# Pads between value-block tiles: moving twelve SBUF tiles under the 512-column products of an encoder block

## The chip, the core and the metric

The kernel runs on one core of one Trainium2 chip. The metric is the device time of one execution in microseconds (us). TensorE is PE in the profile (its loads of stationary operands are listed apart as PEld), VectorE is DVE, ScalarE is ACT, GpSimd is POOL, SyncE is SP.

## The reference, cut to what matters

One encoder block over 1024 tokens of width 1024. A normalised input `h` is multiplied by one wide matrix `w_in`; its columns feed three mixers (dilated windows, grouped-query attention, attention into a memory) and three gates each; the results are merged and projected once more.

```python
h = rms_norm(x, g_pre[layer])
a_qkv, bq, bk, bv, mq, ga, gb, gm, mg = jnp.split(h @ w_in[layer], split_at, axis=-1)
...
merged = gates[:, :, 0] * ya + gates[:, :, 1] * yb + gates[:, :, 2] * ym
out = merged @ w_out[layer]
x = x + rms_norm(out, g_post[layer])
```

Everything below is about `h @ w_in`: how the operands of a part of that product lie in SBUF.

## The kernel before, in words

Each factor of a float32 product is split into a high and a low part, and a product is three matmuls: high by high, high by low, low by high. A large product is cut once more, into 2 by 2 blocks that are combined by a Strassen-like scheme: seven products (A11, A12, S2, S3, S4, S1, A22 by B11, B21, T2, T3, B22, T1, T4), where S1 to S4 are sums of weight blocks and T1 to T4 differences of token blocks. One matmul takes 128 rows by 128 columns of a stationary operand, which a load (LDWEIGHTS) puts into the array beforehand, and streams 512 columns of a moving operand past it ("a product of 512 columns"), or 256 columns in some stages.

The "mega stage" runs from about 450 to 1050 us and has three loops. The first (line 1225) makes two thirds of the value projection: token blocks are stationary, weight blocks of 512 columns move. The second (line 1276) makes the last third in the same way with 256 columns. The third (`pair_product`, matmuls on line 1315) makes 25 pairs of units: weight blocks are stationary, token blocks of 512 columns move. A pair has seven block products of 12 matmuls (four k times three passes), so the third loop has 25 x 7 x 12 = 2100 matmuls. In this whole stage the order on every engine is written out by hand (`tc.manual_schedule`), and PE has the matmuls of one block product after the other in its queue. While one matmul streams, the load of the next matmul's stationary operand runs.

The pool `vb` lies at the right end of SBUF and holds, in order of declaration, the twelve tiles of `Rows` (4096 bytes per partition each: A21, A22, A11, A12, S1, S2, two each, named vA210 to vS21), then `vv`, `vy`, `vot`, `vgt`, `vrt`, `kT3x`. In the first loop the twelve tiles hold raw weight blocks, which are split into other tiles before a matmul reads them. Later their places are used again:

- `KT_PLACE` (line 1020) puts the split token blocks T3 (k = 0, 1) into vA220 and vA221 and T1 into vA110, vA111, vA210, vA211; they are stationary in the second loop and moving in the third.
- `k_block` (line 1073) puts the split weight blocks S2, S1, S3, A22, S4 of the third loop into vS10, vS11, vS20, vS21 in turn; they are stationary there.
- `k_own` (line 1063) splits A11 and A12 of the third loop into `wh` and `wl`, which lie elsewhere.
- `k_load` (line 1044) lands every second pair's raw weights in vA120 and vA121, which VectorE, ScalarE and GpSimd read.

The built program gives each tile its byte address within a partition. What matters here is the remainder of that address by 512 bytes, the size of one loaded operand's row (128 columns of 4 bytes). Before the change the tiles of all operands of the stage's matmuls, moving and stationary, have the remainder 480. "Distance" is, below, the start of the operand being loaded for the next matmul minus the start of the operand streaming in this one, modulo 512; all 2099 steps from one matmul to the next in the third loop, 335 in the second and 335 in the first have the distance 0. Elsewhere the kernel has pads already: one of 448 bytes ahead of the tiles xk (line 236; the memory operands mh and ml of line 526 take their places, remainder 416) and one of 64 bytes ahead of the tiles of the memory attention (line 557; mqh and mql, remainder 32). There, products of 256 columns have distances of 64.

Of the kernel before, what the change touches and what calls it, by code (L numbers as in the profile page):

```python
# [8 lines left out]
F32 = mybir.dt.float32  # L9
# [8 lines left out]
P = 128  # L18
# [15 lines left out]
def block(ctx: ExitStack, tc: tile.TileContext, x, xT, memT, cst, msk, bcst, tabA, gpost,  # L34
# [183 lines left out]
    def pool(name, side="left"):  # L218
        p = tc.tile_pool(name=name, bufs=1, side=side, reuse_waits="tile")
        return p, p.__enter__()  # L220
# [681 lines left out]
    vbp, vb = pool("vb", "right")  # L902
# [7 lines left out]
    class Rows:  # L910

        def __init__(self, nm):
            self.t = [vb.tile([P, 2, 512], F32, name=f"v{nm}{z}") for z in range(2)]

        def __getitem__(self, at):
            return self.t[at[1] // 2][:, at[1] % 2]
# [1446 lines left out]
```

## Time and profile before

| what | value |
|---|---|
| median of the runs of the kernel before | 1369.76 us (1369.28 to 1370.23, 2 runs) |
| the profiled execution's own time | 1369.01 us |
| its span, first to last instruction | 1367.2 us |
| granted TensorE clock | 0.998 |
| PE busy / DVE / ACT / POOL | 98% / 74% / 48% / 42% of the span |
| line 1315 on PE, share of the chain that ended last | 35% |

PE's busy time counts overlapping matmuls once. A matmul's record lasts longer than the distance from its start to the next one's start, since matmuls are pipelined; the rate of a stretch is therefore read from starts, or from the count of matmuls in a window: a window of length W that touches n records of length L holds (W + L)/n per matmul.

### The profile page before, as it was taken

What the parts mean: (1) busy time and instruction counts of PE and PEld (TensorE: products, weight loads), DVE (VectorE), ACT (ScalarE), POOL (GpSimd) and SP (SyncE); (2) the same over time, 40 slices, a digit from 0 to 9 for tenths busy, and PEclk for the clock granted to TensorE, in tenths of its full rate; (3) what the DMA queues carried; (4) which work ended last, traced back from release to release, by engine and by line L of the source; (5) the groups of instructions that cost most, each with busy time, mean ns of one, the idle gap of its engine ahead of it and who ended that gap; (6) DMA issues with size and microseconds to landing.
All of it is one profiled execution on the core that took longest, in us unless ns stands there. A gap on an engine that the chain in (4) does not pass through costs nothing.

```text
span 1367.2 us, 22887 instructions
## 1 busy us (share of the span) xinstructions
PE 1346.3 (98%) x8303; PEld 1087.8 (80%) x8303; DVE 1016.8 (74%) x1836; ACT 655.3 (48%) x1388; POOL 579.4 (42%) x443
## 2 busy tenths in 40 slices
PE   8999999999999999999999999999999999999997
PEld 7899986666666788988888888888888778768886
DVE  7868677777777498767777776687787666768977
ACT  7544465656655445333333343333335676763332
POOL 0516702676676200244465554565553134662003
PEclk9999999999999999999999999999999999999999
DMA  7356532322244579514333333322337778986455
GB/s 253 109 170 231 179 110 92 103 79 93 74 132 141 210 226 285 158 61 139 101 115 117 108 123 123 116 96 92 106 123 262 229 216 236 273 228 228 149 186 185
DMA packets 125490, 213.81 MB, mean 156 GB/s; under 512 B 32481, under 2 KB 64577, under 8 KB 125377
## 3 DMA queue, kind: packets, MB, share of 16 engines
q1 hardware_dynamic: 116064, 198.42, 45.6%
q10 hardware_dynamic: 9312, 13.93, 2.8%
q8 instruction: 65, 1.06, 0.3%
q14 instruction: 49, 0.39, 0.1%
HBM read 145.92 MB, written 66.38 MB: 155 GB/s over the span
## 4 chain that ended last, share of the span: by engine, by line
PE 81%; DVE 6%; DMA 5%; ACT 3%; issue 2%; POOL 2%; SPq 1%; DVEq 0%; ACTq 0%; POOLq 0%
PE s L1315 35%; PE d L1904 6%; PE s L2128 4%; PE ov L810 3%; PE sc L2046 3%; PE s L1276 3%; PE d L132 3%; PE d L130 3%; PE d L128 3%; PE s L1588 2%; PE tr L776 2%; PE s L794 2%; PE s L795 2%; DMA vrt<-rld 2%; PE d L2128 2%
## 5 line engine op out<-in xcount | busy, mean ns | idle before, releaser
L801 POOL TENSOR_TENSOR bl<-bl,bp 128x512 f32<-128x512 f32 x96 | 133.2, 1388 | 54.1 <-ACT bp L797 48.6
L1315 PE MATMUL s<-hh,vS 128*128 128x512 f32 x400 | 131.3, 390 | 0.0
L1315 PE MATMUL s<-vA,vS 128*128 128x512 f32 x450 | 106.1, 390 | 0.0
L91 DVE TENSOR_TENSOR vS<-vot,vS 128x512 fp32r<-128x512 f32 x75 | 89.4, 1193 | 19.9 <-ACT vS L90 19.9
L1315 PEld LDWEIGHTS s<-vA,vS 128*128 128x128 f32 x450 | 84.5, 188 | 17.5
L797 ACT ACTIVATE bp<-s 128x512 f32<-128x512 f32 x128 | 75.6, 596 | 43.8 <-PE s L795 42.7
L777 DVE TENSOR_REDUCE bn<-tr 128x1 f32<-128x512 f32 x128 | 84.9, 683 | 13.3 <-PE tr L776 11.9
L132 PE MATMUL d<-hh,wl 128*128 128x512 f32 x224 | 89.8, 401 | 0.4 <-DVE wl L91 0.4
L128 PE MATMUL d<-hh,wh 128*128 128x512 f32 x224 | 89.2, 398 | 0.0
L130 PE MATMUL d<-hl,wh 128*128 128x512 f32 x224 | 89.1, 398 | 0.0
L1315 PEld LDWEIGHTS s<-hh,vS 128*128 128x128 f32 x400 | 75.2, 188 | 15.5
L1600 ACT ACTIVATE pra<-pra,sts 128x192 f32<-128x192 f32 (+1 forms) x176 | 72.4, 414 | 13.2 <-DVE sts L1599 12.9
L1315 PE MATMUL s<-hh,wl 128*128 128x512 f32 x200 | 78.2, 391 | 0.0
L1315 PE MATMUL s<-hl,wh 128*128 128x512 f32 x200 | 78.0, 390 | 0.0
L1315 PE MATMUL s<-hh,wh 128*128 128x512 f32 x200 | 78.0, 390 | 0.0
L1315 PE MATMUL s<-hl,vS 128*128 128x512 f32 x200 | 77.9, 390 | 0.0
L1599 DVE CUSTOM_DVE_ANT_0 pra<-s,mask 128x192 f32<-128x192 f32 (+1 forms) x192 | 48.9, 309 | 34.1 <-PE s L1588 20.1
L1059 POOL TENSOR_TENSOR vot<-wr 128x512 f32<-128x512 f32 x13 | 22.2, 1707 | 112.3 <-DMA wr<-in_wu 112.3
L1319 ACT ACTIVATE vv<-s 128x512 f32<-128x512 f32 x50 | 29.9, 598 | 82.0 <-PE s L1315 48.1
L810 PE MATMUL ov<-bp,VS 128*64 128x512 f32 x256 | 58.5, 599 | 0.0
L1059 POOL TENSOR_TENSOR vot<-vot,vA 128x512 f32<-128x512 f32 x12 | 19.3, 1606 | 89.3 <-DVE vS L91 89.3
L128 PEld LDWEIGHTS d<-hh,wh 128*128 128x128 f32 x224 | 42.3, 189 | 13.2 <-issue 5.5
(626 smaller groups left out, 4007.0 us busy)
## 6 DMA issues: line engine op xcount, KB each, us to landing
wr<-in_wu SPq DMA_DIRECT2D x40, 512.0 KB
vA<-in_wu SPq DMA_DIRECT2D x24, 512.0 KB
qkd<-ko SPq DMA_DIRECT2D x96, 128.0 KB
wl<-thd SPq DMA_DIRECT2D x24, 512.0 KB
wos<-os SPq DMA_DIRECT2D x12, 512.0 KB
wr<-in_wbr SPq DMA_DIRECT2D x24, 256.0 KB
aq<-qkd SPq DMA_DIRECT2D x12, 512.0 KB
ak<-qkd SPq DMA_DIRECT2D x12, 512.0 KB
```

The costliest lines, as they stand in the source:

```text
L91: V.tensor_tensor(dst_l, src, dst_h.bitcast(F32), op=OP.subtract)
L128: PE.matmul(dst, wh[:, k, :], hh[k][:, t], start=k == 0, stop=False)
L130: PE.matmul(dst, wh[:, k, :], hl[k][:, t], start=False, stop=False)
L132: PE.matmul(dst, wl[:, k, :], hh[k][:, t], start=False, stop=k == 7)
L777: fp["last"] = V.tensor_reduce(st[i]["n"][:, j, c:c + 1], s, axis=AX.X, op=OP.min)
L797: A.activation(pp, s, AF.Exp, scale=-1.0)
L801: G.tensor_tensor(lsum[i % 2], lsum[i % 2], pp, op=OP.add)
L810: PE.matmul(o[e * 64:e * 64 + 64], VS[:, kt, kv], d.pop(kt), start=kt < 2, stop=kt >= NT - 2)
L1315: PE.matmul(BANK[n, c], a, b, start=k == 0 and q == 0 and not more, stop=k == 3 and q == 2, skip_group_check=c in "XW")
L1600: A.activation(src, src, AF.Exp, scale=-1.0, bias=bias, accum_out=sts[:, 1, h, T:T + 1])
L1904: PE.matmul(ps_, a, b, start=k == 0 and q == 0, stop=k == 3 and q == 2)
L2128: PE.matmul(dst[:, e[0]:e[1]], a, b, start=k == 0 and q == 0, stop=k == 3 and q == 2)
```

## The change

After each of the twelve tiles a small tile is allocated that nothing writes or reads: 32 bytes per partition after eleven of them, 384 bytes after vS11. Since the pool ends at a fixed place, the tiles declared later keep their addresses and the twelve move down: vS21 by 32 bytes, vS20 by 64, vS11 by 448, vS10 by 480, vA121 by 512, vA120 by 544, vA111 by 576, vA110 by 608, vA221 by 640, vA220 by 672, vA211 by 704, vA210 by 736.

```diff
     class Rows:
 
         def __init__(self, nm):
-            self.t = [vb.tile([P, 2, 512], F32, name=f"v{nm}{z}") for z in range(2)]
+            self.t = []
+            for z in range(2):
+                self.t.append(vb.tile([P, 2, 512], F32, name=f"v{nm}{z}"))
+                vb.tile([P, 96 if (nm, z) == ("S1", 1) else 8], F32, name=f"pad{nm}{z}")
```

No instruction is added, taken out or moved on any engine or queue, and no wait differs; the two programs differ in addresses alone. Distances of the built program after the change, counted over steps from one matmul to the next:

| loop (columns) | 0 | 32 | 64 | 96 to 288 | 288 to 448 | 448 (64 below) | 480 (32 below) |
|---|---|---|---|---|---|---|---|
| third, line 1315 (512) | 617 | 312 | 292 | 357 | - | 257 | 264 |
| second, line 1276 (256) | 263 | 0 | 0 | - | 72 | - | 0 |
| first, line 1225 (512) | 287 | 0 | 0 | - | 48 | - | 0 |

Within one block product of the third loop the distance stays the same or nearly so; it changes between block products.

## The prediction

> **What bounds the kernel now.** I read the chain that ended last, limited to the third loop of the mega stage, then the windows by stage, then who waited for whom there, and last single starts of matmuls.
>
> The chain from 572 to 1000 us:
>
> ```profile
> 2 pieces in order of time: start us, us, what
> 571.93 0.36 PE s L1276 x3
> 572.29 427.87 PE s L1315 x1886
> ```
>
> It is one unbroken piece of PE: 1886 matmuls in 427.87 us, 226.9 ns each, with no other engine in it. The windows of the same stretch, and two inside it (busy us and count per engine, in the order PE, PEld, DVE, ACT, POOL):
>
> ```profile
> 572.00:1000.00 428.00, 428.00 (x1890) 354.18 (x1889) 322.33 (x342) 157.36 (x248) 225.22 (x135) 1.00 0.35 111
> ...
> 580.00:780.00 200.00, 200.00 (x884) 165.46 (x883) 148.44 (x158) 73.55 (x115) 101.68 (x61) 1.00 0.35 111
> 780.00:980.00 200.00, 200.00 (x883) 165.51 (x882) 149.43 (x158) 73.51 (x114) 104.86 (x64) 1.00 0.34 108
> ```
>
> PE is busy throughout at the full granted clock (1.00); DVE works 322 of 428 us, ACT 157, POOL 225. (200 us + 0.39)/884 is 226.7 ns per matmul, in both halves alike. The other engines wait for PE or for one another; the longest waits there of ACT and POOL, each from its own list:
>
> ```profile
> ACT vS L90 <- PE s L1315: 85.0, 32, 4.8
> ```
>
> ```profile
> POOL vot L1059 <- DVE vS L91: 209.2, 54, 8.4
> ```
>
> So a nanosecond more or less per matmul of line 1315 goes into the time in full, up to the slack of DVE (106 us of 428), and nothing that the other engines do is late for PE. The question is only what the address of an operand does to the distance from one matmul's start to the next.
>
> **The change part by part.** Nothing is issued more or less, so there are only prices per product, and the trace of before has no steady run of 512-column products at a distance other than 0. I bound them by the 256-column products, where it has both.
>
> Durations by line, first of the second value loop (256 columns, distance 0), then of the memory keys (256 columns, distance mostly 64), then of the third loop (512 columns, distance 0); min/median/max in ns:
>
> ```profile
> L1276 PEld LDWEIGHTS s<-wh,hl x64: 187/193/193, 531.8 to 571.8; 128*128 128x128 f32 x64
> L1276 PE MATMUL s<-wh,hl x64: 282/284/284, 531.9 to 571.9; 128*128 128x256 f32 x64
> ```
>
> ```profile
> L526 PEld LDWEIGHTS d<-ml,wh x64: 187/188/193, 56.0 to 79.6; 128*128 128x128 f32 x64
> L526 PE MATMUL d<-ml,wh x64: 276/277/283, 56.1 to 79.7; 128*128 128x256 f32 x64
> ```
>
> ```profile
> L1315 PEld LDWEIGHTS s<-vA,vS x450: 187/188/188, 580.1 to 1041.2; 128*128 128x128 f32 x150
> L1315 PE MATMUL s<-vA,vS x450: 388/390/390, 580.3 to 1041.5; 128*128 128x512 f32 x150
> ```
>
> And the starts: a window that holds line 1276 alone, and eleven consecutive matmuls of line 526:
>
> ```profile
> 535.00:555.00 20.00, 20.00 (x169) 20.00 (x168) 13.88 (x19) 10.61 (x17) 0.00 (x0) 1.00 0.79 240
> ```
>
> ```profile
> 59.33 0.28 PE L526 MATMUL d<-mh,wh 128*128 128x256 f32 x1
> ...
> 60.46 0.28 PE L526 MATMUL d<-ml,wh 128*128 128x256 f32 x1
> ```
>
> At distance 0 a 256-column product takes (20 us + 0.284)/169 = 120.0 ns, at 64 it takes 1.13 us/10 = 113 ns; the loads at distance 0 are 4 to 5 ns longer (193 against 188). So addresses do seem to matter, by 7 ns, where the load of 128 columns and the stream of 256 both fill the whole step (PEld is busy 20.00 of 20.00 us in that window). Two things speak against carrying this over to 512 columns. There, the load has slack: PEld is busy 165.46 of 200 us, and its record is 188 ns, the short value, at distance 0. And 226.7 ns for 512 columns is twice 113 ns for 256 to within the rounding: 0.443 ns per column in both. I read that as a floor per column on which the 512-column products already stand at distance 0.
>
> One rule of the Trainium skill bears on this: "TensorE: Matmul & The Clock Gate", section "Part 2: What happens when you issue a matmul", says that TensorE has two independent SBUF read ports, so that loading the next weights takes no read bandwidth from the running matmul. By that rule the sum is zero for every distance. The 512-column rows agree, as far as they go; the 120 against 113 ns at 256 columns do not, unless something other than the distance separates those lines.
>
> The terms, each against the profiled execution's 1369.01 us (span 1367.2 us; the median of the runs, 1369.76, is 0.75 us above it):
>
> 1. Line 1315, 617 of 2099 steps keep the distance 0: nothing. 1482 steps change. Lower end: each gains what the 256-column products show, 7 ns, 1482 x 0.0067 = 9.9 us (with 120.0 - 113.3). Upper end: each is as slow as 512-column products are after a disturbance (next rows), 5.8 ns, 8.6 us lost. I take 0: the floor per column is the nearest row, being the same products on the same line.
>
> 2. Changes of distance between block products, new in this stage. The nearest rows are after a break of another kind, two transposes at 86.10 us between products of 512 columns, all at distance 0:
>
> ```profile
> 86.10 0.38 PE L514 MATMUL tr<-cs,kvt 128*128 128x128 f32 x2
> 86.24 0.48 PE L128 MATMUL d<-hh,wh 128*128 128x512 f32 x1
> 86.55 0.40 PE L130 MATMUL d<-hl,wh 128*128 128x512 f32 x1
> ...
> 88.41 0.39 PE L128 MATMUL d<-hh,wh 128*128 128x512 f32 x1
> ```
>
> The eight steps from 86.55 to 88.41 us take 232.5 ns each: 46 ns in all above 226.7 before the products settle. The other row is a change of distance itself, from 0 to 64 and to the memory scores:
>
> ```profile
> 173.57 0.39 PE L132 MATMUL d<-hh,wl 128*128 128x512 f32 x1
> 173.80 0.39 PE L128 MATMUL d<-hh,wh 128*128 128x512 f32 x1
> 174.03 0.28 PE L110 MATMUL s<-kmh,mqh 128*128 128x256 f32 x1
> ```
>
> The product at 173.80, during which an operand 64 bytes off is loaded, takes 0.23 us like the one before it. So a change costs between 0 and 46 ns; some 150 of the 175 block products end in one. I take 10 ns, near the second row since it is a change of distance and the first is not: +1.5 us, ends 0 and 7.
>
> 3. Line 1276: 72 of 335 steps leave the distance 0. At best each falls from 120.0 to 113.3: -0.5 us, at worst nothing; I take -0.5. Line 1225: 48 steps, at 7 ns at most 0.3 us either way; I take 0.
>
> 4. The other engines read and write the same tiles at other remainders. Two sources at one remainder cost DVE nothing that can be seen, 692 ns against 684 ns with one source in PSUM:
>
> ```profile
> L199 DVE TENSOR_TENSOR fth<-d,rb 128x512 f32<-128x512 f32 x20 | 13.7, 684 | 5.2 <-PE d L132 5.1
> ...
> L1008 DVE TENSOR_TENSOR vot<-vot,vrt 128x512 f32<-128x512 f32 x8 | 5.5, 692 | 2.4 <-DMA vrt<-rld 2.3
> ```
>
> And DVE has 106 us of slack in the stage, so I take 0. It would show only if DVE's work grew by a third.
>
> Sum: 0 + 1.5 - 0.5 + 0 = +1.0 us, from 1369.8 (the median) to about 1371 us.
>
> **The rivals.**
>
> *The products gain.* If the second part of a 512-column step's overhead comes from loads that meet the stream at distance 0, as in line 1276, all 1482 steps fall to 220.0 ns: 1369.8 - 9.9 - 0.5 = 1359.4 us. For it: 120.0 against 113 ns. Against it: the load's short record at 512 columns, the equal price per column, and the step at 173.80. Its price cannot be much more: 512 columns at 220 ns would already be below the per-column price of any row here. By the same page of the Trainium skill, section "Back-to-back issue gap", a step is N/2.4 + 2.5 ns, an estimate of 215.8 ns for 512 columns; the sum by that, for all 1482 steps, would be 16 us less, near 1354 us. No run here shows such a step.
>
> *The products lose.* At some distances load and stream collide all through the load, and the products stay where they are after a break: 232.5 instead of 226.7 ns. For it: the trace shows that 512-column products have such a slower way of running at the same clock, and twelve products per block are hardly more than the eight that settling took. Against it: the step at 173.80. With 5.8 ns for 1482 steps, and settling at its upper end of 7 us already contained in that, it gives 1369.8 + 8.6 = 1378 us. It decides from an average of 1.5 ns per step on, where it outweighs the rounding of my terms. To be slower by over 2% (27.4 us; about what a measurement of this kernel can tell from no change) it would need 18.5 ns per step, three times what any row shows in a run of products.
>
> *A new wait.* Were the stage faster, ACT or DVE could become late; with DVE at 75% and gains of at most 2% of the stage, this doesn't decide, and I give it no chance of its own.
>
> **How the numbers follow.** The forecast, no price at 512 columns and a little at the changes (1368 to 1373 us): 0.50. The products gain, wholly or in part (1354 to 1367 us): 0.18. The products lose (1374 us and more): 0.32, most of it up to 1381 us (6.7 ns for 1482 steps and 1.5 us of changes), 0.04 beyond 2%. The range runs from 1360 us, nearly the full gain, to 1381 us; about 0.14 lies outside. Faster by over 2% would need 18.5 ns per step below 226.7, hence 208 ns, for which no row speaks: 0.01. Slower by over 2%: 0.04. Within 2%: 0.95.
>
> **What would show it.** Right: windows of 200 us in the third loop again hold 883 or 884 matmuls, the records of line 1315 stay at 390 and 188 ns, and no stretch of PE's chain is replaced by another engine's. A gain shows as some 890 to 905 per window and records near 383 ns; a loss as 860 to 880 and records of 394 to 398 ns. If only certain pairs of tiles shift (vA with vS, say), the distance sets the price, and my floor per column is wrong. If line 1276 does not change for its 72 steps, the distance was not what separates 120 from 113 ns. What would make the prediction wrong above all is that the even spacing of line 1315 hangs on every operand having the same remainder, so that the mixture costs more than any single distance.

## The result: 0.7% slower

| | before | after |
|---|---|---|
| median of the runs | 1369.76 us (1369.28 to 1370.23, 2 runs) | 1378.57 us (1378.21 to 1378.92, 2 runs) |
| ratio | | 1.0072, 95% interval 1.0055 to 1.0088 |
| profiled execution, span, clock | 1369.01 us, 1367.2 us, 0.998 | 1378.92 us, 1377.1 us, 0.998 |

The time lies in the predicted range, but not where the forecast put it (1371 us): it came out at the 1378 us of the rival "the products lose". Three lines were added ahead of the loops, so line 1315 is now 1318, 1276 is 1279 and 1225 is 1228.

The windows of the profile after, the same stretches as before (us, then busy time and count of PE, PEld, DVE, ACT, POOL, then clock):

```profile
572.00:1000.00 428.00, 428.00 (x1857) 348.08 (x1857) 310.83 (x336) 153.81 (x243) 219.40 (x132) 1.00 0.34 107
580.00:780.00 200.00, 200.00 (x868) 162.58 (x867) 143.89 (x155) 71.34 (x112) 99.86 (x60) 1.00 0.34 109
780.00:980.00 200.00, 200.00 (x868) 162.67 (x867) 143.50 (x155) 73.93 (x117) 101.14 (x61) 1.00 0.34 107
535.00:555.00 20.00, 20.00 (x170) 20.00 (x169) 13.76 (x18) 10.59 (x17) 0.00 (x0) 1.00 0.79 237
```

868 products where 883 or 884 were: (200 + 0.39)/868 = 230.9 ns per product instead of 226.7, at the same clock, with PE never idle. The other engines did less in the stretch, since they wait for PE. The chain of the same stretch, after:

```profile
571.99 0.48 PE s L1279 x4
572.47 427.64 PE s L1318 x1852
```

Still one piece of PE with nothing else in it. The waits there, of ACT and of POOL, after:

```profile
ACT vS L90 <- PE s L1318: 87.8, 31, 4.9
```

```profile
POOL vot L1062 <- DVE vS L91: 209.6, 51, 8.6
```

The wait of ACT was 85.0 us before. The prediction's line for POOL covers 570 to 1010 us; from 572 to 1000 us, the window used here, it was, before:

```profile
POOL vot L1059 <- DVE vS L91: 201.8, 53, 8.4
```

Both wait for the same things as before, 3 and 8 us longer; no new wait came. Nor did VectorE slow down on the moved tiles. Its costliest group in the same stretch, before and then after (busy us, mean ns):

```profile
L91 DVE TENSOR_TENSOR vS<-vot,vS 128x512 fp32r<-128x512 f32 x68 | 80.5, 1185 | 17.1 <-ACT vS L90 17.1
```

```profile
L91 DVE TENSOR_TENSOR vS<-vot,vS 128x512 fp32r<-128x512 f32 x67 | 76.1, 1137 | 17.1 <-ACT vS L90 17.1
```

So the time went into the products themselves. Their records by operands, min/median/max in ns and first and last start, before:

```profile
L1315 PE MATMUL s<-hh,vS x400: 388/390/390, 588.5 to 1048.3; 128*128 128x512 f32 x134
L1315 PE MATMUL s<-hh,wh x200: 387/390/397, 572.1 to 1031.5; 128*128 128x512 f32 x100
```

and after:

```profile
L1318 PE MATMUL s<-vA,vS x450: 388/394/404, 580.6 to 1050.0; 128*128 128x512 f32 x150
L1318 PE MATMUL s<-hh,vS x400: 388/394/398, 588.9 to 1057.0; 128*128 128x512 f32 x134
L1318 PE MATMUL s<-hh,wh x200: 389/389/398, 572.3 to 1039.8; 128*128 128x512 f32 x100
```

Products with a sum (vS) as weights went from 390 to 394 ns; those with A11 and A12 (wh), which kept the distance 0, went from 390 to 389. The loop lasts from 572.1 to 1048.3 us before, from 572.3 to 1057.0 after: 476.2 and 484.7 us, 8.5 us of the 8.8 us between the medians.

The start of each product, taken from the trace in ns and joined with the addresses of its operands in the built program, gives the step by distance (mean ns from one start to the next, line 1318):

| distance, bytes | 0 | 32 | 64 | 96 | 128 | 160 | 192 | 224 | 256 | 288 | 448 | 480 |
|---|---|---|---|---|---|---|---|---|---|---|---|---|
| steps | 617 | 312 | 292 | 57 | 76 | 75 | 54 | 36 | 38 | 21 | 257 | 264 |
| ns | 227.9 | 232.9 | 232.7 | 232.8 | 232.4 | 233.4 | 232.0 | 230.8 | 231.5 | 231.1 | 229.2 | 233.4 |

Against 226.67 ns (the settled step before) the steps at other distances than 0 lose 8.13 us in all and those at 0 0.78 us; the loop before lost 0.37 us by the same measure: 8.13 + 0.78 - 0.37 = 8.5 us.

### The profile page after: what moved, and what is told of

The parts are those of the page before. It is cut to its first block, busy times and chain, and to the rows that moved or that the text cites. A ratio compares the mean times of both kernels' runs of the same rounds, so it can differ in the third digit from the quotient of the medians.

```text
span 1377.1 us, 22887 instructions
## 1 busy us (share of the span) xinstructions
PE 1354.5 (98%) x8303; PEld 1086.8 (79%) x8303; DVE 1012.2 (73%) x1836; ACT 654.1 (47%) x1388; POOL 579.4 (42%) x443
## 4 chain that ended last, share of the span: by engine, by line
PE 83%; DVE 5%; DMA 4%; ACT 3%; POOL 2%; issue 2%; SPq 1%; DVEq 0%; ACTq 0%; POOLq 0%
PE s L1318 35%; PE d L1907 5%; PE s L1228 4%; PE s L2131 4%; PE ov L810 3%; PE sc L2049 3%; PE s L1279 3%; PE d L132 3%; PE d L130 3%; PE d L128 3%; PE tr L776 2%; PE s L794 2%; PE s L795 2%; PE s L1591 2%; PE d L2131 2%
## 5 line engine op out<-in xcount | busy, mean ns | idle before, releaser
L91 DVE TENSOR_TENSOR vS<-vot,vS 128x512 fp32r<-128x512 f32 x75 | 85.6, 1142 | 19.9 <-ACT vS L90 19.9
L776 PE MATMUL tr<-KS,QH 128*128 128x512 f32 x128 | 51.5, 402 | 1.5 <-DVE bn L777 0.7
```

The lines of the kernel that those rows point to most:

```text
L91: V.tensor_tensor(dst_l, src, dst_h.bitcast(F32), op=OP.subtract)
L776: PE.matmul(s, QH[:, kv * 4 + j], KS[:, kv, c * 512:c * 512 + 512], start=True, stop=True)
```

## The experiments

Theory A: the distance between the operand being loaded and the one streaming sets the step of a 512-column product, all along a run. B: no distance costs by itself, but their mixture or their changes do, as the end of the prediction feared. C: the moved tiles cost something that has nothing to do with distances. D, put up later: the loaded operand's own address costs. Other letters are explained where they stand. Where a time comes from one run it scatters like the single runs of before, which reached from 1366.4 to 1371.3 us; the verdict is then the step, read from starts.

**All tiles moved, no distance changed.** Pads of 512 bytes, after four of the twelve tiles, so that the twelve move by 512 to 2048 bytes:

```diff
+    PADS = {('A22', 1): 128, ('A12', 1): 128, ('S1', 1): 128, ('S2', 1): 128}
...
-            self.t = [vb.tile([P, 2, 512], F32, name=f"v{nm}{z}") for z in range(2)]
+            self.t = []
+            for z in range(2):
+                self.t.append(vb.tile([P, 2, 512], F32, name=f"v{nm}{z}"))
+                if (nm, z) in PADS:
+                    vb.tile([P, PADS[nm, z]], F32, name=f"pad{nm}{z}")
```

> The twelve tiles move (by 512 to 2048 bytes), but by multiples of 512 bytes, so every distance stays 0. Theory A (the distance modulo 512 between the operand being loaded and the operand streaming sets the step of a 512-column product; 0 is the price of 226.7 ns): 1369.8 us within 1.5, 883 or 884 matmuls per 200 us in the third loop. Rival B (the change of distance from one block product to the next is what costs, as a settling time; one distance kept throughout settles to 226.7 ns): the same, 1369.8. Rival C (the place of the tiles matters in another way, through other engines or the DMA): about 1378.

1368.30 us against 1368.06 us, ratio 0.9999 (0.999 to 1.0008). Its window:

```profile
580.00:780.00 200.00, 200.00 (x883) 165.34 (x883) 148.11 (x158) 73.32 (x115) 101.33 (x61) 1.00 0.35 111
```

883 products again. Moving the tiles costs nothing as long as the remainders stay equal, so C falls as far as it rests on the move alone. That other remainders cost through other engines is not excluded by this run; the run with both moved, below, speaks to that.

**One distance for all sums, 64 bytes.** The same code with other pads (in floats); 1500 steps at 64, the 599 of A11 and A12 at 0:

```diff
-    PADS = {('A22', 1): 128, ('A12', 1): 128, ('S1', 1): 128, ('S2', 1): 128}
+    PADS = {('A12', 1): 16, ('S2', 1): 112}
```

> All four weight-block tiles of the third loop stand 64 bytes above every token tile, so 1500 of 2099 steps have the distance 64 and 599 keep 0. Theory A: 1500 steps at the 233.5 ns that this distance shows in the changed kernel (231 and 236 in turn), 1500 x 6.8 = 10.2 us and about 1 us of settling: 1381 us, about 861 matmuls per 200 us. Rival B: fewer changes of distance than in the changed kernel (some 100 instead of 150), and each block settles: 1370 to 1375 us, and the same as the run with 448. Rival C: no forecast apart from 1378.

1379.17 us, ratio 1.0079 (1.0064 to 1.0094), a little more than the mixture cost:

```profile
580.00:780.00 200.00, 200.00 (x863) 161.94 (x862) 142.70 (x156) 70.17 (x111) 99.87 (x60) 1.00 0.35 110
```

863 products. The step at 64 is 233.17 ns; at 0, behind such blocks, it is 229.25 ns. No mixture of many distances is needed. Changes between 0 and 64 remain in this run; the run with the other weights moved, below, has long stretches without any.

**One distance, 448 bytes** (64 the other way):

```diff
+    PADS = {('A12', 1): 112, ('S2', 1): 16}
```

> The same 1500 steps, 64 bytes below instead of above (distance 448). Theory A: 229.1 ns per step as in the changed kernel (226, 229, 232 in turn), 1500 x 2.4 = 3.6 us and about 1 us of settling: 1374 us, about 876 matmuls per 200 us. Rival B: the same as the run with 64, 1370 to 1375 us.

1370.61 us, ratio 1.0017 (1.0008 to 1.0027):

```profile
580.00:780.00 200.00, 200.00 (x878) 164.56 (x877) 148.15 (x158) 72.92 (x115) 101.78 (x61) 1.00 0.34 109
```

The step is 228.89 ns, a pattern of 226, 229, 232 that repeats; A had expected 229.1. The time is 2.5 us above before and not the 4 us or so that A allowed, since the steps at 0 stayed at 226.75 ns: no settling came on top. The time by itself would have suited B as well (1370 to 1375 us); B falls by the run before, which it expected to be equal to this one. In this loop 64 bytes above and 64 below cost different amounts.

**The other weights moved, the sums left alone.** The tiles wr, wh and wl move by 64 bytes, which also gives the dense products of the first 60 us one constant distance of 64:

```diff
+    wp.tile([P, 16], F32, name="padw", bufs=1)
...
+    wp.tile([P, 112], F32, name="padx", bufs=1)
```

> The tiles wr, wh, wl are moved by 64 bytes for the whole kernel and nothing else: the dense 512-column products (lines 128 to 132 and 1904 of the kernel before), the 599 steps of A11 and A12 and most of line 2046 get the distance 64, 193 steps of line 1225 and all 335 of the 256-column line 1276 get 448; line 526 goes from 64 to 128. Theory A: the steps of A11 and A12 go to 233.5 ns (+4.1 us), the dense ones that run undisturbed too (some 300, +2.0), lines 2046 and 2128 +1.3, line 1225 +0.5, line 1276 falls to 113.3 ns (-2.2): 1375.5 us, from 1373 to 1378. Rival B: long runs at one distance settle to 226.7 ns, so nothing is lost and line 1276 gains: 1367.5 to 1370 us. In the dense stretches of the first 60 us the starts decide: 233 ns apart by A, 227 by B.

1376.69 us, ratio 1.0059 (1.0044 to 1.0074). Dense products before, first and last of 19 in a row:

```profile
32.19 0.39 PE L128 MATMUL d<-hh,wh 128*128 128x512 f32 x1
...
36.27 0.39 PE L128 MATMUL d<-hh,wh 128*128 128x512 f32 x1
```

and in this run, first and last of 42 in a row:

```profile
39.61 0.39 PE L131 MATMUL d<-hl,wh 128*128 128x512 f32 x1
...
49.18 0.39 PE L129 MATMUL d<-hh,wh 128*128 128x512 f32 x1
```

4.08 us/18 = 226.7 ns before, 9.57 us/41 = 233.4 ns here, and no settling over 41 steps that all have the same distance. That is A and excludes B. In the third loop the 599 steps at 64 take 232.92 ns and the 1500 at 0 take 227.67. One expectation missed: the 256-column products of the second loop, all at 448 in this run, take 117.8 ns and not 113.3; before it was 120.0. And 448 has no single price at 512 columns either: in the first loop of this run the first 120 steps at 448 take 233.3 ns without settling, while later blocks at the same distance settle to the 228.9 ns of the run before.

**Which distances cost: three scans in whole block products.** The four slots of the sums get four distances; 599 steps stay at 0.

```diff
+    PADS = {('A12', 1): 24, ('S1', 0): 16, ('S1', 1): 16, ('S2', 0): 8, ('S2', 1): 64}
```

> The four slots of the sums are moved so that 384, 372, 372 and 372 of the third loop's products of 512 columns have their weights at 96, 160, 224 and 256 bytes (modulo 512) from the streamed operand; 599 stay at 0. A, the distance alone sets the step: the means per distance come out as they did in the mixture, 232.8, 233.4, 230.8 and 231.5 ns, within 0.7 ns, also where a block holds one distance throughout, and the time is that of before plus about 384 x 6.1 + 372 x (6.7 + 4.1 + 4.8) ns, 8.1 us, near 1376 us. B, a mixture of distances costs and one distance by itself doesn't: steps of 226.7 to 228 ns and a time within 2 us of before.

```diff
+    PADS = {('A12', 1): 72, ('S1', 0): 16, ('S1', 1): 8, ('S2', 0): 8, ('S2', 1): 24}
```

> The same with 288 bytes (384 products), 352, 384 and 416 (372 each); 599 at 0. The mixture had only 288 with many products, at 231.1 ns; 448 by itself took 228.9. A: each distance has its own step, 288 at 231.1, the others not below 228 ns and not above 234; a time from 1371 to 1378 us. C, the price falls gradually toward 448, as though only the part of a row by which load and stream overlap counted: 352 below 288, 384 below 352, 416 at 229 to 230.

(C in this expectation is another theory than the one above: a price that falls gradually.)

```diff
+    PADS = {('A12', 1): 32, ('S1', 0): 16, ('S1', 1): 32, ('S2', 0): 40, ('S2', 1): 8}
```

> 128 bytes (384 products), 192, 320 and 480 (372 each) in whole blocks, 599 at 0. A: no further free distance, 128 between 231.5 and 233.5 ns, 192 at 231 to 233, 320 at 231 to 234, 480 at 233 to 234, and a time of 6.5 to 9.5 us above before. C2, remainders modulo 128 count (0, 128, 256 and 384 are one class): 128 at 227 to 228 ns, and 2 us less than A says; against C2 stand the 232.4 ns of 384 in whole blocks.

1376.27, 1379.62 and 1379.27 us in one run each, against 1368.3, 1368.3 and 1368.1 us. The windows of the second scan and of the third:

```profile
580.00:780.00 200.00, 200.00 (x864) 162.04 (x863) 143.17 (x155) 70.99 (x112) 99.88 (x60) 1.00 0.34 108
```

```profile
580.00:780.00 200.00, 200.00 (x867) 162.48 (x866) 143.64 (x155) 70.65 (x112) 99.75 (x60) 1.00 0.34 109
```

Mean step by distance, 372 or 384 steps each:

| bytes | 96 | 128 | 160 | 192 | 224 | 256 | 288 | 320 | 352 | 384 | 416 | 480 |
|---|---|---|---|---|---|---|---|---|---|---|---|---|
| ns | 233.8 | 232.8 | 233.4 | 230.7 | 233.2 | 227.3 | 233.1 | 232.9 | 234.0 | 232.4 | 233.6 | 233.0 |

The gradual fall toward 448 isn't there (288, 352 and 416 are alike), and 128 and 384 are no free classes. A holds against B and the gradual fall, but its figures missed in places: 256 bytes came out free, not at the 231.5 ns of the mixture, where it stood in runs of one to three products only; 224 took 233.2 ns, not 230.8, 288 took 233.1, not 231.1, and 96 was 1.0 ns above its mean in the mixture. A mean over short runs in a mixture isn't the price of a distance. The first scan's 1376 us came out as expected because these misses cancel; the second scan lies above the 1371 to 1378 us expected (its third loop alone lasts 10.8 us longer than before), and the third, 11.2 us above before, lies above the 6.5 to 9.5 us, 9.3 us of it in the third loop. At 192 the mean hides two steady ways: block products whose stream begins with vA110 or with aq take 233.3 ns, the other three kinds about 229, the same ones in every pair.

**Half a unit for all: 256 bytes**, to test the surprise:

```diff
+    PADS = {('A12', 1): 64, ('S2', 1): 64}
```

> All 1500 products whose weights are sums stand at 256 bytes from their stream, 599 at 0. In the scan of 96, 160, 224 and 256 bytes the 372 products at 256 took 227.3 ns, while the mixture of the changed kernel had 231.5 in runs of one to three products. A with a free half unit (0 and 256 are one class): 227 to 227.5 ns, 881 to 883 products per 200 us, a time 0.3 to 1 us above before, ratio 1.000 to 1.001. A as first put (only equal remainders modulo 512 are free, and 227.3 was an accident of the pattern): 231 to 232 ns, 6.5 us or more above before, ratio from 1.005.

1368.18 us against 1368.08 us, ratio 1.0002 (0.9992 to 1.0012). The window and the records:

```profile
580.00:780.00 200.00, 200.00 (x884) 165.31 (x883) 149.72 (x159) 73.81 (x116) 101.80 (x61) 1.00 0.33 109
```

```profile
L1321 PE MATMUL s<-vA,vS x450: 389/389/389, 578.9 to 1040.1; 128*128 128x512 f32 x150
```

All 1500 steps at 256 bytes average 226.67 ns. So for these products 0 and 256 are free alike.

**Distances below 32 bytes: 4, 8, 16 and 24.** The four slots become tiles of 1032 columns with the weights 1, 2, 4 or 6 floats in:

```diff
...
-        t = vb.tile([P, 1024], R, name=("vS10", "vS11", "vS20", "vS21")[next(s_turn) % 4])
+        z = next(s_turn) % 4
+        o = (1, 2, 4, 6)[z]
+        t = vb.tile([P, 1032], R, name=("vS10", "vS11", "vS20", "vS21")[z])[:, o:o + 1024]
...
```

> Weights at 4 bytes (384 products), 8, 16 and 24 (372 each) from the streamed operand's remainder; 599 at 0. A1, the price hangs on whole units of 32 or 64 bytes, and below 32 bytes there is none: all four within 0.7 ns of 227.7, and the time of before within 1 us. A2, only exactly equal remainders are free: 231 to 234 ns at all four, a time 6 to 9 us above before. Between these, a row that starts off a unit touches one unit more, and 4, 8, 16 and 24 bytes are alike at whatever price.

1375.41 us in one run, 7.1 us above before; 232.4, 230.4, 230.7 and 230.7 ns at 4, 8, 16 and 24 bytes. A1 falls: there is no free zone of 32 bytes, a single float off already costs. A2 has the time, but its 231 to 234 ns came at 4 bytes only. At 16 bytes there are two steady ways. A block product with hh and hl (token blocks split into high and low part) as stream, and then the end of the next one at the same distance, with kT as stream:

```profile
646.44 0.39 PE L1323 MATMUL s<-hh,vS 128*128 128x512 f32 x1
...
648.70 0.39 PE L1323 MATMUL s<-hl,vS 128*128 128x512 f32 x1
```

```profile
661.60 1.56 PE L1323 MATMUL s<-kT,vS 128*128 128x512 f32 x6
```

The first has 10 steps in 2.26 us, 226 ns; the second 5 steps in 1.56 - 0.39 = 1.17 us, 234 ns. Over the whole loop each of the five kinds of block product keeps its own way in all pairs: two at 226.67 ns, three at 233. The addresses modulo 2048 are the same in both kinds, so the remainder alone doesn't decide. Whether it is something that the preceding products leave behind or a higher part of the address stays open.

**The stream moved instead of the load.** Tiles of T1 and T3 move by 64 bytes, the weights stay where they were:

```diff
+    PADS = {('A12', 1): 16}
```

> Here the streamed token blocks T1 and T3 move (their six tiles, by 64 bytes downward), and the weights stay: 450 of the third loop's steps have the load at 64 bytes from the stream, 1649 at 0. A, the distance between load and stream sets the step: the 450 take 232 to 234 ns, about 2.8 us more in all, near 1371 us in one look; windows of 200 us hold 878 to 880. D, it is the loaded operand's own address that costs (in all runs so far with a price the weights had been moved): the 450 stay at 226.7 to 228 ns and the time at that of before.

1370.36 us in one run, against 1369.20 us in one run of before. The records:

```profile
L1321 PE MATMUL s<-vA,vS x450: 394/394/394, 578.8 to 1043.2; 128*128 128x512 f32 x150
L1321 PE MATMUL s<-hh,vS x400: 389/389/389, 587.1 to 1050.0; 128*128 128x512 f32 x134
```

The 450 products of the moved streams take 394 ns without exception (step 233.33 ns), the same weights with the unmoved stream 389. D falls: weights at their old address cost 6.7 ns as soon as the stream stands elsewhere. The windows hold 877, one below what was expected; steps at 0 behind a change took up to 236 ns. The third loop lasts 3.2 us longer than before and the second 0.5 us less; the 1.2 us between two single runs lie within their scatter.

**Both moved together**, all twelve tiles by 448 bytes:

```diff
+    PADS = {('S2', 1): 112}
```

> All twelve tiles move together by 448 bytes (modulo 512), weights as well as T1 and T3. The 450 products of T1 and T3 with the sums then have load and stream at equal remainders again, distance 0, though both stand elsewhere; the 1050 products of the other token blocks with the same weights have the distance 64. A: the 450 take 226.7 to 228.5 ns, the 1050 take 232 to 234, about 6.6 us more, near 1375 us. D, the loaded operand's own address: all 1500 take 232 to 234 ns, 9.5 us more, near 1378 us.

1376.38 us in one run, against the same 1369.20 us. The records are the mirror image of the last run:

```profile
L1321 PE MATMUL s<-vA,vS x450: 387/389/398, 580.5 to 1050.4; 128*128 128x512 f32 x150
L1321 PE MATMUL s<-hh,vS x400: 392/394/398, 588.7 to 1057.4; 128*128 128x512 f32 x134
```

Load and stream at the same new remainder: 389 ns in the median; unmoved stream: 394. What counts is the distance between the two and not the address of either, which settles A against D from the other side. It also leaves no room for the rest of C: the same moved weights are cheap or dear by the stream that they meet. The 1050 steps at 64 average 233.04 ns. The 450 at 0 average 229.03, half a nanosecond above the 228.5 expected at most: they settle over nine steps after each change (233, 236, 224, 231, 236, 228, 232, 231, 227 in one block), about 37 ns a change. Changes of distance do cost, but as a second and smaller term.

**The one gain on offer: 256 columns only.** The second loop's weights for A11, S2, S4, and the high parts of S3 and S1, moved to 448 (208 of 335 steps); every 512-column step stays at 0:

```diff
...
-        h, l = wslot(0), wslot(1)
+        if nm in ("A11", "S2", "S4"):
+            h, l = [vb.tile([P, 1040], R, name=f"vS2{z}")[:, 16:1040] for z in range(2)]
+        else:
+            h, l = v3.tile([P, 1024], R, name="w3h") if nm in ("S3", "S1") else wslot(0), wslot(1)
...
```

> Only products of 256 columns get a distance: 208 of the 335 of the second value loop have their weights at 448 bytes, all of the 512-column products keep 0. A: the 208 steps fall from 120.0 ns to one of the two values seen at 448, 113.3 (a gain of 1.4 us) or 117.8 (0.5 us); the time is 0.5 to 1.4 us below before, a ratio from 0.9990 to 0.9996. B, no gain from distances at all in this loop, since something else holds it: the ratio is 1.000 and the 208 steps stay at 120 ns.

1368.30 us against 1368.32 us, ratio 1.0000 (0.9991 to 1.0009): no gain. Records of a moved and of an unmoved kind, and the one wait of PE in that loop:

```profile
L1291 PE MATMUL s<-vS,hh x64: 279/280/282, 531.4 to 559.7; 128*128 128x256 f32 x64
...
L1291 PE MATMUL s<-wh,hh x32: 277/283/290, 537.0 to 571.5; 128*128 128x256 f32 x32
```

```profile
PE s L1291 <- DVE wl L91: 0.3, 1, 0.3
```

B has the time right and its reason wrong: the wholly moved blocks do run at 117 or 118 ns instead of 120.0. But S3 and S1, where a third of the steps kept the distance 0, show five steps of 116 to 118 ns and then one of 127 or 128, and at 559.92 us PE waits for a split that came later in this arrangement. With that wait the 208 moved steps average 119.9 ns, and the loop takes 40.35 us, 0.15 more than before. None of the layouts was faster than the kernel before.

## Why the prediction was right in its range and wrong in its reason

The range held because it took in the rival "the products lose", which had a chance of 0.32; the forecast itself, about 1371 us (1368 to 1373, a chance of 0.50), did not come.

**Term 1, line 1315 at no price: failed.** The 1482 changed steps lose 8.13 us, 5.5 ns each, close to the upper end that the term named (5.8 ns, 8.6 us). What the prediction held for no price, and against the rivals:

- *The floor per column.* That 226.7 ns is twice 113 ns was read as a floor on which the products stand whatever the distance. 226.7 is indeed the lowest settled mean in any run here, but a floor says nothing about what lies above it. And the 256-column rows, from which the term took its end of a gain, have the opposite sign: in the run with moved streams the second loop has 119.9 ns at 0 and 113.5 at 448, the third 227.0 at 0 and 233.3 at 64; in the run with all twelve tiles moved, the second loop has 117.8 at 64 too.
- *The slack and the short record of the load.* The load's record was 188 ns at 226.7 ns per step, and it is 188 ns now. From the page of the profile after:

```profile
L1318 PEld LDWEIGHTS s<-vA,vS 128*128 128x128 f32 x450 | 84.5, 188 | 20.0
```

The load has more slack than before (busy 162.58 of 200 us, 165.46 before), and the products are slower all the same. The load's record doesn't show the loss; the matmul's does (390 to 394).
- *The step at 173.80 us.* One step with a load 64 bytes off took 0.23 us, and was held against both rivals. Where sums at 64 follow products at 0, the first step at 64 takes 225 or 226 ns and the second 236, so that step can't show the price. This is no rule for all first steps: in the kernel after, the first step at 32 or 480 takes 235 ns, and in the run with moved streams the first at 64 takes 233 or 234.

**The rival "the products lose": right** in what the products do, in size (232.5 ns expected, 232.2 on average measured) and in time (1378 us). That load and stream collide, as it put it, is not shown. The closeness of its size is partly luck: its row, the eight slow steps after two transposes, is a settling at distance 0 that ended, and no steady pace at another distance. The rule of the Trainium skill that the prediction weighed ("TensorE: Matmul & The Clock Gate", "Part 2: What happens when you issue a matmul": two independent read ports, so a load takes nothing from the running matmul) doesn't hold here to the last 3%: 226.67 ns become 233.33 when nothing but the relative address of load and stream changes.

**The rival "the products gain": fell.** No step of 512 columns below 226.67 ns on average over a settled run appeared at any of the distances tried, nor does any run show the 215.8 ns worked out there from the Trainium skill, whose section "Back-to-back issue gap" gives that formula for an isolated matmul.

**Term 2, changes of distance at 1.5 us (0 to 7): of the right size.** The 617 steps at 0 lose 0.78 us, some 16 ns for each of the 50 blocks of A11 and A12. Inside the other blocks changes can't be told from the price of the distance.

**Term 3, line 1276 at -0.5 us: right in sign, too large.** The second loop went from 40.19 to 39.98 us, -0.2 us: its 72 steps fell to between 113 and 120 ns and not all to 113.3. The 48 steps of line 1225, taken at 0, lost 0.3 us, the end that the term named.

**Term 4, the other engines at nothing: held.** The third loop's products account for 8.5 of the 8.8 us, PE waited for no other engine in it, and VectorE's costliest group took 1137 ns instead of 1185. The Trainium skill's "SBUF — State Buffer", section "Who interferes with whom", says that TensorE shares its read ports with no other engine. Nothing in the runs speaks against that: with the same instructions on all other engines the step is 226.67 ns at 256 bytes and 233.2 at 64.

Shown by these runs: the distance between load and stream decides whether these products keep the pace of 226.67 ns; 0 and 256 bytes always did once settled, and at 16, 192 and 448 bytes the same distance had two paces. Not shown: why. That the two reads meet in the same part of the memory would fit, but no view shows a read, and a collision that is worst at 352 bytes, absent at 256 and undecided at 16 isn't explained by it.

## What to carry to other kernels

Where a run of float32r products of 512 columns bounds the time, lay the tiles of both operands out so that their addresses agree modulo 256 bytes: in these runs 32 bytes of distance cost 2.7% of the step, and 256 or 512 bytes nothing. Products of 256 columns wanted the opposite (120.0 ns at equal remainders, 113 to 118 at 64 and 448), so neither rule carries over to another width unless the starts there show it. And price a change of state by a run of steps in that state, not by its first step.

## What the runs showed of the hardware that was not expected

- The step of a 512-column product against the distance of the next load from the stream: 226.67 ns at 0 and 256 bytes, 228.9 or 233.3 at 448, 230.4 to 232.4 at 4 to 24, 230.7 at 192, 232.4 to 234.0 at all others tried.
- The steps at a distance repeat in patterns, stable over dozens of products: 233, 233, 234 or 231, 236 at 64; 226, 229, 232 at 448; 230, 232, 238 at 160 and 416. Some distances have two steady ways: 16 bytes 226.67 or 233, 192 bytes 228.9 or 233.3, 448 bytes 228.9 or 233.3; 256-column products at 448 113.5 (moved streams) or 117.8 (moved weights).
- Several steady means are whole multiples of 6.667 ns: 226.67 is 34 of them, 233.33 is 35, 120.0 is 18, 113.33 is 17.
